# The recurrence over chunks is moved from beside attention to beside the input projections

## The chip, the cores and the metric

The kernel runs on one core of a Trainium2 chip. The metric is the device time of one execution in microseconds (us). The core has five engines that take their own instruction queues in order: TensorE (PE, its weight loads are shown as PEld), VectorE (DVE), ScalarE (ACT), GpSimd (POOL) and SyncE (SP), which here only issues DMAs. Matrix products land in PSUM, eight banks, and ScalarE or VectorE must take them out of there.

## The reference

One layer on 2048 tokens of width 1024. A normalised input goes through one combined projection; half of the columns feed eight heads of softmax attention with a forget bias, the other half eight heads of a recurrence (RWKV-7). Both results side by side go through an output projection, and a gated feed-forward layer follows.

```python
u = rmsnorm(h, attn_norm_pre)
proj = u @ w_in
o_fox = forgetting_attention(fq, fk, fv, ff, fox_forget_bias)
# recurrence, S is 64x64 per head, one step per token:
S = S * w_t + (S a_t) b_t^T + v_t k_t^T
y_t = S r_t
# its norm per head and its gate
o_rwkv = (norm(y) * ln_w + ln_b + bonus) * g
h = h + rmsnorm(concat(o_fox, o_rwkv) @ w_out, attn_norm_post)
h = h + rmsnorm((silu(z @ w_gate) * (z @ w_up)) @ w_down, ffn_norm_post)
```

## The kernel before

**Stages.** The 2048 tokens are four blocks of 512. `phase_a` makes the input projections of a block in turn, 27 products of 128 columns each: three small latent ones (`stage_l`), twelve for the recurrence (`stage_pre`, four pairs of heads with three each) and twelve for attention (`stage_fox`). A product (`proj`) is 24 matmuls of 512 columns: operands are split into a high and a low part, and three products of parts are added (`mm3`). The weights come new for every product and block: a load of 512 KB (`wraw`, L187), a cast on ScalarE (`wh`, L217), a subtraction on GpSimd (`wl`, L218), each with three buffers. The normalised and transposed input of a block (`uh`, `ul`) has two buffers, one for each of two blocks in turn. `stage_pre` leaves five operands of the recurrence for each chunk of 64 tokens in memory (`A5`, stored as `scr["a5"]`), and `stage_solve` inverts the chunks' triangular matrices on VectorE and leaves them in `scr["td"]`.

`phase_b` runs three lanes side by side: the recurrence (`rwkv`), attention (`attention`), and the output projection of the blocks that are done (`Mix.block`, with `Mix.norm` behind it). The feed-forward part (`Ffn`) comes last; the output projection of the fourth block runs beside its first loads.

**The recurrence.** It works in groups of two chunks and four heads; four groups are a half block (four of the eight heads), two half blocks a block, 32 groups in all. A group has ten steps: `tt` twice (transposes, L669, L670), `gram` twice (G, L681, masked by VectorE at L684), `x` (X, L692), `u` (U, L700), `c` twice (C, L708) and `y` twice (Y, L725), where VectorE multiplies the state (`SI`, L726) and ScalarE copies the result into `yg` (L728). Each step ends with copies out of PSUM by ScalarE or VectorE. Steps of two neighbouring groups are interleaved by the list `ORDER`; a dash marks a step of the group before. Every group loads its operands (`A`, L636, `PL`, L637) and its inverses (`TD`, L647) through SP's queue. After four groups `post_norm` gives norm and gate of two pairs of heads in three steps each, called "tail" in `ORDER`.

**Attention.** A unit is one head and 256 queries (J counts them, 0 to 7; two units of a head for each block of 512), 64 units in all, 16 in a block. `scores` makes S (L886, L887), adds the bias while taking the maximum on VectorE (L894) and the exponential on ScalarE (L900). `values` transposes the result (L929), splits it (L935, L937) and multiplies by V into O (L947). VectorE adds O's two halves into `ot` (L953), which has one buffer; GpSimd scales it and stores it (L954, L955). The scores of a unit run beside the values of the one before.

**What sets the order.** `weave` takes generators and steps through them in proportion to the length given with each one (a third number scales it); what comes first in the program has the higher priority. The framework then plans the order on each engine, and inserts the waits. `behind` gives the output projection a much lower priority. A block's output projection starts when the recurrence has finished the block (`rdone`) and attention has begun the next one (`adone`).

Of the kernel before, what the change touches and what calls it, by code (L numbers as in the profile page):

```python
# [10 lines left out]
F32 = mybir.dt.float32  # L11
# [4 lines left out]
ALU = mybir.AluOpType  # L16
# [20 lines left out]
ORDER = ("t0", "-c0", "tail", "t1", "-c1", "tail", "g0", "-y0", "g1", "load", "-y1", "x", "tail", "u", "tail")  # L37
# [117 lines left out]
def phase_a(k, tc, ins, scr):  # L155
# [5 lines left out]
    with ExitStack() as ctx:  # L161
# [17 lines left out]
        spare = p1.tile([128, 2, D], F32, tag="A5", name="spare", bufs=2)  # L179
# [14 lines left out]
        fetched = [fetch(L0 + 128, 128), fetch(L0 + 256, 72), fetch(L0, 128)]  # L194
# [17 lines left out]
        def weights(c0, n):  # L212
            raw = fetched.pop(0) if fetched else fetch(c0, n)
# [32 lines left out]
        def start_block(b, blk):  # L246
            blk.b, blk.t = b, slice(b * BT, (b + 1) * BT)
            blk.uh = pu[b % 2].tile([128, NJ, BT], F32R, tag="uh", name="uh")
            blk.ul = pu[b % 2].tile([128, NJ, BT], F32R, tag="ul", name="ul")

        def flip(blk, tt, xt):
            for jj in range(2):
# [4 lines left out]
                cols = slice(tt * 128, (tt + 1) * 128)  # L257
                oh = blk.uh[:, jj * 4:jj * 4 + 4, cols]
# [3 lines left out]
        def first_u(blk):  # L262

            start_block(0, blk)
            for i, xt in enumerate(first_x):
# [12 lines left out]
        def stage_u(b, blk):  # L278
            start_block(b, blk)
            prev = None  # L280
# [68 lines left out]
        def stage_pre(blk, p, nd, pl):  # L349
# [5 lines left out]
            A5 = p1.tile([128, NCB, 5, CL], F32, tag="A5", name="A5", bufs=2)  # L355
# [154 lines left out]
        def stage_fox(blk, i):  # L510
# [3 lines left out]
            oh = p2.tile([128, BT], F32R, tag="fo", name="oh", bufs=3)  # L514
            ol = p2.tile([128, BT], F32R, tag="fo", name="ol", bufs=3)
# [11 lines left out]
            else:  # L527
                vt = p2.tile([128, BT], F32, tag="fo", name="vt", bufs=3)
# [4 lines left out]
                vs = p2.tile([128, 4, 2, 2, HD], F32R, tag="vs", name="vs")  # L533
# [21 lines left out]
        weave((stage_l(blk), 3))  # L555
# [12 lines left out]
        weave((solve, NSOLVE), (fox, 6))  # L568


def rwkv(k, tc, ctx, ins, scr):

    nc = tc.nc
    pa = ctx.enter_context(tc.tile_pool(name="r_a", bufs=2))
    cp = ctx.enter_context(tc.tile_pool(name="r_const", bufs=1))
    p2 = ctx.enter_context(tc.tile_pool(name="r2", bufs=2))
    ps_rw = ctx.enter_context(tc.tile_pool(name="r_rw", bufs=2, space=PSUM))

    pg = ctx.enter_context(tc.tile_pool(name="r_g", bufs=1, side="right"))
    g1 = pa.tile([128, HW], F32, tag="bv0", name="g1", bufs=1)  # L580
    nc.scalar.dma_start(out=g1, in_=ins["rwkv_g_up"][0][0:128, :])
    g2 = pa.tile([128, HW], F32, tag="bv1", name="g2", bufs=1)
# [1046 lines left out]
```

## Time and profile before

| | us |
|---|---|
| median of 3 runs | 3539.27 (3529.62 to 3541.76) |
| the profiled execution | 3532.8 |
| its span | 3531.0 |
| TensorE busy | 3107.4 (88%) |
| VectorE busy | 2424.2 (69%) |
| ScalarE busy | 1542.2 (44%) |
| GpSimd busy | 1511.0 (43%) |
| mean granted TensorE clock | 0.922 |

The granted clock is the share of TensorE's full rate that it was given; in the records it has two levels, 1 (2.4 GHz) and one half (1.2 GHz), and a mean between them says how much of a stretch was at which. Matmuls are pipelined, so that the length of one record is longer than the distance to the next. Busy shares over the whole span mix the stages, which have different limits; a stage has to be read in its own window.

### The profile page before, as it was taken

To read this page: it belongs to the slowest core of one execution; us is meant where nothing else is said; L and a number is where in the kernel's file an instruction comes from. 1 tells how busy PE (TensorE), PEld (TensorE's weight loads), DVE (VectorE), ACT (ScalarE), POOL (GpSimd) and SP (SyncE) were. 2 spreads that over 40 slices of the span, in tenths; PEclk is the share of its full clock that TensorE was granted. 3 is DMA by queue.
4 is the path that set the end of the run, shared out by engine and by line. 5 is a ranking of instruction groups with operands and counts; after the bars stand their busy time and mean duration, and the time that the engine had idled before them with its cause. 6 is when DMAs were issued, how large, how long until landed. Compare 5 with 4: busy or idle time off the path is not lost. (4 is left out here: it accounts for less than half of the span.)

```text
span 3531.0 us, 48961 instructions
## 1 busy us (share of the span) xinstructions
PE 3107.4 (88%) x16657; PEld 2566.7 (73%) x16657; DVE 2424.2 (69%) x5285; ACT 1542.2 (44%) x2966; POOL 1511.0 (43%) x1203
## 2 busy tenths in 40 slices
PE   7999999994678889898888779999999999997895
PEld 5777777773567778687777657888878888775674
DVE  6877666664245666657666557687685556999898
ACT  5444444332445555555655343333333333543432
POOL 3343444442322232223223245343453334887776
PEclk9999999997688989898998789999999999998898
DMA  4766566577546666656664563243232222322321
GB/s 127 189 169 174 152 168 174 158 174 172 106 108 131 159 147 158 133 157 178 169 172 117 154 212 117 101 150 114 84 119 84 84 78 107 144 98 93 143 96 72
DMA packets 509198, 480.31 MB, mean 136 GB/s; under 512 B 143780, under 2 KB 410070, under 8 KB 506902
## 3 DMA queue, kind: packets, MB, share of 16 engines
q1 hardware_dynamic: 473734, 432.47, 43.0%
q0 software_dynamic: 11008, 24.20, 2.7%
q10 hardware_dynamic: 24208, 20.52, 1.9%
q8 instruction: 133, 2.18, 0.3%
q14 instruction: 115, 0.94, 0.1%
HBM read 350.25 MB, written 126.81 MB: 135 GB/s over the span
## 5 line engine op out<-in xcount | busy, mean ns | idle before, releaser
L1196 POOL TENSOR_TENSOR wl<-fraw,wh 128x512 fp32r<-128x512 f32 x132 | 186.5, 1414 | 474.5 <-ACT wh L1192 458.1
L218 POOL TENSOR_TENSOR wl<-wraw,wh 128x1024 fp32r<-128x1024 f32 (+1 forms) x108 | 262.2, 2430 | 297.3 <-ACT wh L217 292.8
L1440 POOL TENSOR_TENSOR dop<-draw,dop 128x512 fp32r<-128x512 f32 x210 | 330.3, 1602 | 92.8 <-ACT dop L1438 53.8
L1192 ACT CAST wh<-fraw 128x512 fp32r<-128x512 f32 x308 | 187.4, 618 | 387.7 <-PE gp L77 198.3
L76 PE MATMUL mm<-uh,wh 128*128 128x512 f32 (+1 forms) x864 | 348.7, 404 | 1.4 <-DVE ol L522 1.4
L78 PE MATMUL mm<-uh,wl 128*128 128x512 f32 (+1 forms) x864 | 346.8, 401 | 0.0
L77 PE MATMUL mm<-ul,wh 128*128 128x512 f32 (+1 forms) x864 | 346.1, 401 | 0.0
L76 PE MATMUL dps<-dop 128*128 128x512 f32 x624 | 251.6, 408 | 57.8 <-ACT acc L1535 27.8
L1438 ACT CAST dop<-draw 128x512 fp32r<-128x512 f32 x280 | 155.7, 622 | 234.5 <-DVE draw L1446 152.7
L77 PE MATMUL dps<-dop 128*128 128x512 f32 x624 | 248.1, 398 | 1.2 <-POOL dop L1440 1.2
L78 PE MATMUL dps<-dop 128*128 128x512 f32 x624 | 246.7, 397 | 0.0
L947 PE MATMUL O<-th,Vs 128*128 128x256 f32 (+1 forms) x672 | 202.1, 355 | 39.4 <-DVE ot L953 19.7
L76 PE MATMUL gp<-za,wh 128*128 128x512 f32 x528 | 210.1, 398 | 15.8 <-ACT za L1192 9.9
L929 PE MATMUL pt<-ident,P 128*128 128x128 f32 x1088 | 191.5, 300 | 31.4 <-DVE tl L937 22.4
L1196 DVE TENSOR_TENSOR wl<-fraw,wh 128x512 fp32r<-128x512 f32 x176 | 157.5, 895 | 85.9 <-ACT wh L1192 82.0
L937 DVE TENSOR_TENSOR tl<-pt,th 128x512 fp32r<-128x512 f32 (+2 forms) x280 | 163.1, 590 | 72.6 <-ACT th L935 68.8
L77 PE MATMUL gp<-za,wh 128*128 128x512 f32 x528 | 208.1, 394 | 2.8 <-DVE za L1196 2.8
L78 PE MATMUL gp<-za,wl 128*128 128x512 f32 x528 | 208.7, 395 | 0.0
L894 DVE CUSTOM_DVE_ANT_0 P<-S,ng 128x512 f32<-128x512 f32 (+3 forms) x288 | 169.4, 596 | 52.5 <-PE S L887 27.7
L1446 DVE TENSOR_TENSOR draw<-draw 128x512 f32<-128x512 f32 x160 | 194.5, 1232 | 5.3 <-POOL dop L1440 4.7
L76 PEld LDWEIGHTS mm<-uh,wh 128*128 128x128 f32 (+1 forms) x864 | 165.8, 192 | 43.4 <-issue 3.8
L900 ACT ACTIVATE P<-P,nmx 128x128 f32<-128x128 f32 (+15 forms) x128 | 154.1, 1205 | 96.7 <-DVE nmx L899 75.7
(362 smaller groups left out, 8568.9 us busy)
## 6 DMA issues: line engine op xcount, KB each, us to landing
wraw<-in_w_in SPq DMA_DIRECT2D x104, 512.0 KB
fraw<-in_ffn_w_gate SPq DMA_DIRECT2D x22, 1024.0 KB
fraw<-in_ffn_w_up SPq DMA_DIRECT2D x22, 1024.0 KB
scr_hid<-s SPq DMA_DIRECT2D x22, 1024.0 KB
draw<-scr_hid SPq DMA_DIRECT2D x22, 1024.0 KB
draw<-in_ffn_w_down SPq DMA_DIRECT2D x22, 1024.0 KB
scr_a<-A SPq DMA_DIRECT2D x16, 1280.0 KB
A<-scr_a SPq DMA_DIRECT2D x64, 320.0 KB
```

Of the source, the lines that this page charges most:

```text
L76: nc.tensor.matmul(out, lhsT=wh, rhs=xh, start=first, stop=False)
L77: nc.tensor.matmul(out, lhsT=wh, rhs=xl, start=False, stop=False)
L78: nc.tensor.matmul(out, lhsT=wl, rhs=xh, start=False, stop=last)
L218: nc.gpsimd.tensor_tensor(wl[:, :, 0:m], raw[:, :, 0:m], wh[:, :, 0:m], op=ALU.subtract)
L894: nc.vector.tensor_tensor_reduce(out=P[:, c0 + a:c0 + e], in0=S[:, a:e], in1=bias, op0=ALU.add, op1=ALU.max, scale=1.0, scalar=-3.0e38, ac ...
L929: nc.tensor.transpose(pt[:, e, qi, :], Ps[qi][:, kb * 128:(kb + 1) * 128], k.ident)
L937: nc.vector.tensor_tensor(tl[:, w[0], w[1]], pt[:, w[0], w[1]], th[:, w[0], w[1]], op=ALU.subtract)
L947: nc.tensor.matmul(O[:, q0 * 128:QB], lhsT=vv, rhs=p[:, e, q0:NQ, :], start=kb == 0 and i == 0, stop=kb == nkb - 1 and i == len(parts) - 1)
L1192: f.nc.scalar.copy(h, x)
L1196: e.tensor_tensor(l[:, c], x[:, c], h[:, c], op=ALU.subtract)
L1440: e.tensor_tensor(r[1][p][i], x, r[0][p][i], op=ALU.subtract)
L1446: V.tensor_tensor(o[p], x[p], y[p], op=op)
```

## The change

The recurrence becomes a class with a generator for each half block, and `phase_a` steps through half block n - 2 while it projects half block n. Half block 6 runs beside the last products of attention's operands, half block 7 in `phase_b`. Norm and gate become a class of their own, `Gates`, which stays in `phase_b` and runs block by block as a lane of its own; between the two, the recurrence's result `yg` goes through memory (`scr["ry"]`). `phase_a` has fewer buffers, in SBUF and PSUM: weights from three to two, the product's PSUM banks and those of the elementwise steps from three to two each, `A5` from two to one, and `uh`, `ul` from two to one: the next block's input is kept unsplit (`us`) and split at the border (`split`). Attention's projections (`stage_foxes`) run in the same half block and no more one half block later, except in the last block, and the latent ones (`stage_l`) at a block's start instead of at the end of the block before. Attention's tiles move to the other side of SBUF.

```diff
-ORDER = ("t0", "-c0", "tail", "t1", "-c1", "tail", "g0", "-y0", "g1", "load", "-y1", "x", "tail", "u", "tail")
+ORDER = ("t0", "-c0", "t1", "-c1", "g0", "-y0", "g1", "load", "-y1", "x", "u")
+ORDER0 = ("load0", "-c0", "-c1", "-y0", "t0", "-y1", "t1", "g0", "g1", "load", "x", "u")
...
-        pu = [ctx.enter_context(tc.tile_pool(name=f"a_u{i}", bufs=1)) for i in range(2)]
-        pw = ctx.enter_context(tc.tile_pool(name="a_w", bufs=3))
+        pu = ctx.enter_context(tc.tile_pool(name="a_u", bufs=1))
+        pw = ctx.enter_context(tc.tile_pool(name="a_w", bufs=2))
...
-        ps_el = ctx.enter_context(tc.tile_pool(name="a_el", bufs=3, space=PSUM))
-        ps_mm = ctx.enter_context(tc.tile_pool(name="a_mm", bufs=3, space=PSUM))
+        ps_el = ctx.enter_context(tc.tile_pool(name="a_el", bufs=2, space=PSUM))
+        ps_mm = ctx.enter_context(tc.tile_pool(name="a_mm", bufs=2, space=PSUM))
...
+        def split(blk):
+
+            operands(blk)
+            for j in range(NJ):
+                nc.scalar.copy(blk.uh[:, j], blk.us[:, j])
+                (nc.vector if j % 2 == 0 else nc.gpsimd).tensor_tensor(blk.ul[:, j], blk.us[:, j], blk.uh[:, j], op=ALU.subtract)
...
-            A5 = p1.tile([128, NCB, 5, CL], F32, tag="A5", name="A5", bufs=2)
+            A5 = p1.tile([128, NCB, 5, CL], F32, tag="A5", name="A5")
...
             for half in range(2):
+                n = b * 2 + half
                 nd = dr.tile([32, CL, CL], F32, tag="nd", name="nd")
-                lanes = [(chain(*(stage_pre(blk, half * 2 + pl, nd, pl) for pl in range(2))), 14), (solve, NSOLVE), (fox, 6)]
+                pre = [stage_pre(blk, half * 2 + pl, nd, pl) for pl in range(2)]
+                if half == 0:
+                    if b > 0:
+                        split(blk)
+                    pre = [stage_l(blk)] + pre
+                if b + 1 < NB:
+                    fox = stage_foxes(blk, half * 6)
+                lanes = [(chain(*pre), 17 if half == 0 else 14), (solve, NSOLVE), (fox, 6)]
                 if half == 1 and b + 1 < NB:
-                    lanes.append((chain(stage_u(b + 1, nxt), stage_l(nxt)), 8))
+                    lanes.append((stage_u(b + 1, nxt), 5))
+                if n >= 2:
+                    lanes.append((rec.half(n - 2), 40))
                 weave(*lanes)
-                solve = stage_solve(nd, scr["td"][b * 2 + half])
-                fox = stage_foxes(blk, half * 6)
+                solve = stage_solve(nd, scr["td"][n])
+                fox = stage_foxes(blk, half * 6) if b + 1 == NB else iter(())
             blk = nxt
-        weave((solve, NSOLVE), (fox, 6))
+        weave((solve, NSOLVE), (fox, 6), (rec.half(NB * 2 - 2), 40))
...
+            if g == NG - 1 and q == 1:
+                for e in range(2):
+                    nc.gpsimd.dma_start(out=o.scr["ry"][i // (2 * NG), half * 2 + e], in_=o.yg[e].rearrange("p g h d -> p (g h d)"))
...
+    def half(o, n):
+
+        NG = o.NG
+        for i in range(n * NG, (n + 1) * NG):
+            for step in ORDER0 if i % NG == 0 else ORDER:
+                lag = step[0] == "-"
+                if step == "load0":
+                    o.load(i)
+                    o.groups.append(o.group(i))
+                elif step == "load":
+                    if i % NG < NG - 1:
+                        o.load(i + 1)
+                        o.groups.append(o.group(i + 1))
+                elif i >= lag:
+                    o.groups[i - lag][step[lag:]]()
+                    yield
...
+    def block(o, b, done):
...
+        for p in range(4):
+            yg = p2.tile([128, NCB // 2, 2, HD], F32, tag="yg", name="yg")
+            nc.sync.dma_start(out=yg.rearrange("p g h d -> p (g h d)"), in_=scr["ry"][b, p])
...
-        weave((recurrence(rdone), NB * (8 * 10 + 13), 0.92), (after(), 560 * T // 2048), (run(adone), n_at))
+        first = chain(*(gates.block(b, rdone) for b in range(NB - 1)))
+        last = chain(rec.half(NB * 2 - 1), rec.flush(), gates.block(NB - 1, rdone))
+        weave((last, 44 + 16, 0.6), (first, 16 * (NB - 1), 0.25), (after(), 560 * T // 2048), (run(adone), n_at))
```

## Rows read from the trace of the kernel before

**Rows 1.** Windows by stage: window, length, busy us of PE, PEld, DVE, ACT, POOL; clock, DMA

```profile
100.00:800.00 700.00, 662.14 (x4085) 531.06 (x4084) 488.52 (x1186) 302.04 (x492) 316.48 (x223) 0.96 0.65 168
837.00:1034.00 197.00, 128.89 (x797) 110.43 (x797) 65.57 (x299) 80.51 (x233) 53.93 (x75) 0.71 0.54 105
1034.00:1212.00 178.00, 147.52 (x985) 131.38 (x985) 106.18 (x392) 95.34 (x230) 48.30 (x71) 0.90 0.61 133
1212.00:1524.00 312.00, 273.64 (x1787) 239.83 (x1788) 199.51 (x640) 174.30 (x370) 87.62 (x106) 0.89 0.62 153
1524.00:1944.00 420.00, 371.69 (x2467) 329.08 (x2468) 272.04 (x858) 236.59 (x485) 122.21 (x134) 0.91 0.56 156
1944.00:2030.00 86.00, 63.56 (x329) 52.30 (x328) 50.14 (x168) 33.31 (x72) 23.35 (x24) 0.74 0.52 154
2030.00:3531.00 1501.00, 1369.68 (x5801) 1102.27 (x5800) 1161.55 (x1531) 562.93 (x987) 815.99 (x533) 0.96 0.32 111
```

**Rows 2.** Timeline, end of attention, recurrence; first feed-forward weight: start, length, what

```profile
1942.82 0.22 PE L947 MATMUL O<-th,Vs 128*128 128x128 f32 x1
...
2004.81 1.97 PE L725 MATMUL Y<-SI,CS 128*128 128x64 f32 x8 [0.74 <-DVE SI L726]
...
2027.66 0.38 SPq L1186 DMA_DIRECT2D fraw<-in_ffn_w_gate  x1
```

**Rows 3.** Waits between 795 and 900 us: who, for whom, total us, times, longest

```profile
PE S L886 <- DMA Q<-scr_qS: 22.0, 2, 20.3
```

**Rows 4.** Timeline of TensorE, one group of the recurrence among other work

```profile
1660.94 0.27 PE L669 MATMUL tt<-ident,A 128*128 128x128 f32 x1
...
1661.38 1.06 PE L708 MATMUL C<-R,UV 128*128 128x128 f32 x8
...
1672.41 1.16 PE L681 MATMUL G<-A 64*128 64x128 f32 x8
...
1677.18 1.00 PE L725 MATMUL Y<-SI,CS 128*128 128x64 f32 x8
...
1683.12 0.73 PE L692 MATMUL X<-UV,R 64*64 64x64 f32 x16
...
1689.19 1.06 PE L700 MATMUL U<-Z,TD 128*128 128x128 f32 x8
```

**Rows 5.** Groups by line, 837 to 2030: count, busy us, mean ns, idle before

```profile
L728 ACT COPY yg<-Y 64x128 f32<-64x128 f32 x128 | 26.7, 257 | 66.7 <-DVE SI L726 66.1
...
L684 DVE TENSOR_TENSOR R<-G,gmask 128x256 f32<-128x256 f32 x128 | 48.1, 417 | 13.6 <-PE G L681 12.2 <-issue 0.6
...
L953 DVE TENSOR_TENSOR ot<-O,ol 64x256 f32<-64x256 f32 x64 | 26.5, 414 | 109.9 <-DMA scr_mixT<-ot 77.0 <-ACT ol L952 18.0 <-issue 7.8
```

**Rows 6.** Weights in the projections: groups by line; waits of SP's queue

```profile
L217 ACT CAST wh<-wraw 128x1024 fp32r<-128x1024 f32 (+1 forms) x108 | 111.4, 1032 | 139.6 <-PE mm L77 72.5 <-issue 31.0 <-POOL Tt L461 15.6
...
SPq L187 <- POOL wl L218: 73.4, 30, 4.4
```

**Rows 7.** Timeline of SP's queue: loads of TD for one group

```profile
960.08 2.75 SPq L647 DMA_DIRECT2D TD<-scr_td  x4
```

**Rows 8.** Windows as in 1; then groups by line: 1367 to 1447, 1447 to 1524

```profile
1367.00:1447.00 80.00, 75.21 (x530) 65.67 (x528) 56.06 (x176) 48.05 (x104) 21.78 (x26) 0.98 0.68 158
1447.00:1524.00 77.00, 58.30 (x347) 51.51 (x348) 47.18 (x167) 37.63 (x76) 14.83 (x21) 0.76 0.55 142
1637.00:1738.00 101.00, 98.71 (x710) 87.48 (x709) 66.99 (x209) 62.18 (x130) 24.32 (x29) 1.00 0.65 179
1738.00:1838.00 100.00, 81.66 (x526) 71.90 (x525) 69.52 (x240) 55.28 (x111) 25.61 (x31) 0.86 0.61 167
...
L725 PE MATMUL Y<-SI,CS 128*128 128x64 f32 x48 | 6.1, 270 | 0.6 <-ACT yg L728 0.6
...
L725 PE MATMUL Y<-SI,CS 128*128 128x64 f32 x24 | 4.7, 365 | 0.0
...
L953 DVE TENSOR_TENSOR ot<-O,ol 64x256 f32<-64x256 f32 x4 | 1.6, 411 | 0.0
```

More of the change, by code (lines that the diff above doesn't have):

```diff
@@ L192, in fetch @@
             return raw
-        fetched = [fetch(L0 + 128, 128), fetch(L0 + 256, 72), fetch(L0, 128)]
+        fetched = {c0: fetch(c0, n) for c0, n in ((L0 + 128, 128), (L0 + 256, 72))}
         wa_h = [cp.tile([128, HW], F32R, name=f"wa_h{i}") for i in range(2)]
@@ new lines, in phase_a, with __init__, bank, load @@
+        weave((solve, NSOLVE), (fox, 6), (rec.half(NB * 2 - 2), 40))
+class Recurrence:
+    def __init__(o, k, tc, ctx, scr):
+        nc = tc.nc
+        o.k, o.nc, o.scr = k, nc, scr
+        o.pa = ctx.enter_context(tc.tile_pool(name="r_a", bufs=2))
+        cp = ctx.enter_context(tc.tile_pool(name="r_const", bufs=1))
+        o.p2 = ctx.enter_context(tc.tile_pool(name="r2", bufs=2))
+        o.ps = ctx.enter_context(tc.tile_pool(name="r_rw", bufs=2, space=PSUM))
+        o.gmask = cp.tile([128, 2, CL], F32, name="gmask")
+        nc.gpsimd.memset(o.gmask, 1.0)
+        for h in range(2):
+            for q in range(2):
+                ap = o.gmask[h * 64:(h + 1) * 64, q, :]
+                nc.gpsimd.affine_select(out=ap, in_=ap, pattern=[[1, CL]], compare_op=ALU.is_gt if q == 0 else ALU.is_ge,
+                                        fill=0.0, base=0, channel_multiplier=-1)
+        o.SI, o.TD, o.UV = [], [], []
+        for half in range(2):
+            t = cp.tile([128, 2, 2, HD], F32, name=f"SI{half}")
+            nc.gpsimd.memset(t[64:128], 0.0)
+            for u in range(4):
+                nc.gpsimd.tensor_copy(t[0:64, u // 2, u % 2, :], k.ident[0:64, 0:64])
+            o.SI.append(t)
+        for i in range(2):
+            t = cp.tile([128, 2, 2, 128], F32, name=f"TD{i}")
+            nc.gpsimd.memset(t, 0.0)
+            o.TD.append(t)
+        for i in range(2):
+            t = cp.tile([128, 2, 2, 2, 128], F32, name=f"UV{i}")
+            nc.gpsimd.memset(t[64:128], 0.0)
+            o.UV.append(t)
+        o.NG = NCB // 2
+        o.groups = []
+    def bank(o, n):
+        return o.ps.tile([128, 4, 128], F32, tag="rw", name=n)
+    def load(o, i):
+        nc, scr, NG = o.nc, o.scr, o.NG
@@ L719, in y @@
             if g == 0 and q == 0:
-                for pr in prs:
-                    pr.yg = p2.tile([128, NG, 2, HD], F32, tag="yg", name="yg")
+                o.yg = [p2.tile([128, NG, 2, HD], F32, tag="yg", name="yg") for e in range(2)]
             Y = bank("Y")[:, 0:2, :].rearrange("p e (h d) -> p e h d", h=2)
@@ L814, in run @@
+            nc.sync.dma_start(out=scr["mixT"][HW + p * 128:HW + (p + 1) * 128, t], in_=om)
             yield
-    return run
+        done[0] = b
 def attention(k, tc, ctx, scr):
@@ L1102, in behind, with phase_b @@
         yield
-def phase_b(k, tc, ins, scr, mix):
+def phase_b(k, tc, ins, scr, mix, rec):
     T = k.T
@@ L1110, in phase_b @@
     with ExitStack() as ctx:
-        recurrence = rwkv(k, tc, ctx, ins, scr)
+        gates = Gates(k, tc, ctx, ins, scr, rec.ps)
         ps_e = ctx.enter_context(tc.tile_pool(name="e_p", bufs=1, space=PSUM))
         run = attention(k, tc, ctx, scr)
-        rdone, adone = [0], [0]
+        rdone, adone = [-1], [0]
         def after():
@@ L1579, in fox_rwkv7_block @@
     constants(k, tc, ctx, ins)
-    phase_a(k, tc, ins, scr)
     NB = T // BT
     with ExitStack() as c2, ExitStack() as ce:
-        mix = Mix(k, tc, ce, ins, scr)
-        phase_b(k, tc, ins, scr, mix)
+        with ExitStack() as cr:
+            rec = Recurrence(k, tc, cr, scr)
+            phase_a(k, tc, ins, scr, rec)
+            mix = Mix(k, tc, ce, ins, scr)
+            phase_b(k, tc, ins, scr, mix, rec)
         ffn = Ffn(k, tc, c2, ins, scr, out[0])
```

207 lines of the change are left out of this document (69 added, 138 removed).

## The prediction

> **What bounds the kernel now.** I read the stretches of the span first, because the shares on the page mix four different stages. [rows 1] has one window for each: the input projections (100 to 800 us), attention over its four blocks of 512 queries (837 to 1034, 1034 to 1212, 1212 to 1524, 1524 to 1944), what is left of the recurrence when attention has ended (1944 to 2030), and the feed-forward part (2030 to 3531). The reader is to look at PE busy and at the granted clock together. I call PE busy times granted clock the *work*, in microseconds at full speed, and work divided by the window's length the *density*. The projections have 662.1 x 0.96 = 636 us of work in 700, a density of 0.91: TensorE bounds them, and no other engine is over 70% (VectorE, 488.5). The five windows from 837 to 2030 have 91.5 + 132.8 + 243.5 + 338.2 + 47.1 = 853 us of work in 1193, a density of 0.715. The worst are the first block (0.46) and the end (0.55); blocks 2 and 3 stand at 0.78 and 0.81. So a microsecond of TensorE work is cheaper to place beside the projections than beside attention, and that is the whole question of this change: TensorE's work is not made less, it is moved to a stage with another density.
>
> Second, the end. The last matmul of attention starts at 1942.82, the last one of the recurrence at 2004.81, and the first load of a feed-forward weight, which needs what attention, recurrence and gate hold, goes out at 2027.66 [rows 2]. These 85 us exist because the recurrence with its gate is the longer of two lanes. Third, the start: TensorE stands still for 20.3 us before attention's first scores, until Q has landed [rows 3].
>
> **What moves, and its work.** The recurrence has 32 groups (8 half blocks of 4). The 28 of half blocks 0 to 6 go beside the projections; the last four, all norms and all gates stay. [rows 4] shows each step's burst at full clock: tt (records 0.11 us apart, eight of them in a group: 0.88), C 1.06 twice, G 1.16 twice, Y 1.00 twice, X 0.73, U 1.06, together 9.1 us. A record lasts 0.27 and the next starts 0.11 after it, so each of the eight other bursts ends some 0.16 after the next could begin: 7.8 us at least. 28 groups are 218 to 255 us; I take 8.6 a group, 240.
>
> **Cost in the projections.** At their own density of 0.91 the 240 us take 240 / 0.91 = 264. Less is possible, if the steps fall into TensorE's idle 38 us of the 700 (bound: 218 less 8 of these 38, 210). The other engines have room: the recurrence's costliest VectorE group is 48.1 us for all 32 groups [rows 5] and it has four such groups, so under 4 x 48.1 x 7/8 = 168 come to the 488.5, and the stretch grows by more. ScalarE is at 43%.
>
> The same edit takes buffers away, since the recurrence's tiles now live through this stage. Raw and split weights go from three buffers to two. Today the weight cast, 1.03 us each, waits 72.5 us in all for TensorE to free a buffer, and the fetch on SP's queue waits 73.4 us in 30 waits for the subtraction that frees its own [rows 6]: the fetch is limited by buffers and not by bandwidth, and one less takes one projection's lead away. I price that at nothing to 0.8 us (most of a cast) for each of the 81 projections of blocks 1 to 3, 0 to 65, and take none, because the cast is short and the moved steps lengthen the time between projections that hides it. The normalised input is now held once: at three block borders ScalarE and VectorE must split the first slice while TensorE waits, a cast of half the weight cast's size, so some 0.52, and a subtraction that takes longer: I allow 3 us each, 9 in all. The 24 casts, some 13 us, lie on a ScalarE with room. Moved past SP's queue are the loads: four of TD take 2.75 us of issue [rows 7], so 28 x 2.75 = 77 and about as much for A and PL; behind them stand weight fetches, and a load that waits for its buffer holds the fetch behind it; this risk is in the 65. The state's output goes out and comes back through memory, 16 tiles of 256 KB; the gate runs a block behind, which hides it. Sum: 264 + 9 = +273, bounds +210 and +338.
>
> **Gain in attention.** 853 - 240 = 613 us of work stay. At the old density of 0.715 they take 857, at 0.70 876. What the density will be no row shows directly, so I look at both sides. For a better one: the two worst windows shrink. The end goes, since four groups and one block's gate are done well before attention ends. Recurrence steps also block the in-order queues of other engines: ScalarE's copy of Y has 66.1 us of waiting for the state's update in front of it [rows 5]. For a worse one: the first block is not short of engines, its VectorE waits 77.0 us over the whole of attention for the store of the unit before, through the one *ot* buffer [rows 5], so there the recurrence was free filling. And the filling of blocks 2 and 3 goes too: [rows 8] has two pairs of neighbouring stretches of four attention units each. With 48 records of Y (three groups) the density is 75.2 x 0.98 / 80 = 0.92; with 24 it is 58.3 x 0.76 / 77 = 0.58, and four units take 77 us instead of 80. In block 3 it is 0.98 against 81.7 x 0.86 / 100 = 0.70, again in the same time. I take 0.70: between the average and the sparse stretches, nearer to the average because the end and the blocked queues are gone. 876 us, a gain of 317, with bounds 0.78 (786, gain 407) and 0.56 (1095, gain 98; worked out below).
>
> **Sum.** 3531 + 273 - 317 = 3487 us of span. The profiled run took 3532.8, 1.8 more than its span, and the median of the runs is 0.18% above it: 3489 x 1.0018 = 3495.
>
> **Rivals,** as spans; a median is 8 us more. *Attention keeps its pace* (slower). Place: attention's blocks 1 to 3, 910 us. Mechanism: with less on TensorE its clock falls, matmuls take twice as long, and four units take what they took. For it: in both sparse stretches of [rows 8] the clock is lower (0.76 and 0.86 against 0.98 and 1.00), and the time the same. Against it: these stretches still carry recurrence steps, norms and gates in the queues of the other engines. Price: first block 175 (the start a little shorter), blocks 1 to 3 still 910, end 10: 1095, gain 98, 3531 + 273 - 98 = 3706. It decides from the point where the gain falls below 273: blocks 1 to 3 over 735, that is four units of block 2 over 63 us. Half-way (0.9 of today's pace) gives 3615.
>
> The Trainium skill, page "TensorE: Matmul & The Clock Gate", section "Why this matters for your kernels", speaks for this rival: it asks to avoid idle gaps between bursts of matmuls, since the array then goes back to half its rate. The clock of 0.76 in the sparser stretch agrees. By that rule alone, with the clock of that stretch and 0.80 busy, 613 us take 613 / 0.61 = 1005, and the change costs 85.
>
> *Both stages do better.* The moved steps fill the projections' idle time (+210) and attention, with the other queues freed, reaches 0.78, block 2's own density today: gain 407. 3531 + 210 - 407 = 3334. For it speak the waits in [rows 5]; against it that the sparse stretches show no faster unit.
>
> *The projections starve.* Two weight buffers don't cover the fetch, and TensorE, the bound there, waits 0.8 us a projection: +338, gain 317 as forecast, 3552. For it: the 73.4 us in [rows 6]; against it: the cast waits for TensorE and not TensorE for the cast.
>
> **How the numbers follow.** Forecast 0.48, own range 3420 to 3550; attention keeps pace or nearly 0.24 (3560 to 3715); both better 0.18 (3340 to 3420); starving 0.10 (3540 to 3590); all as medians. A measurement of this kernel tells about 0.3% from no change, 3529 to 3550 here. Faster: 0.39 of the forecast's, 0.18 and 0.01: 0.58. Same: 0.05 of the forecast's, 0.03 of the third and 0.02 of the first rival: 0.10. Slower: 0.32. For eight in ten the range goes from 3385, a good half of the better case, to 3630, half of the slower one.
>
> **What would show it.** In the profile after, the projections should end near 1110 instead of 837, with a density of about 0.91 from 100 us on; if the stretch is longer and TensorE's idle time there is ended by the weight cast or subtraction, the two buffers are to blame. Attention's last matmul to the first feed-forward weight load should be under 20 us instead of 85. Four units of block 2 should take under 63 us, four of block 3 under 85; if they take 77 and 100 with a clock of 0.8 or less, the slower rival holds. The feed-forward part should be 1501 us as before. The forecast is wrong if the density of either stage moves by over 0.05 from 0.91 and 0.70.

## The result and the profile after

The change makes the kernel slower: a median of 3634.9 us (3619.3 to 3637.9) against 3540.5 for the kernel before, a ratio of 1.0256 with a 95% interval of 1.0211 to 1.0302. The forecast was 3495, within 3385 to 3630. The profiled execution after has a span of 3635.3 us, 104 more than before.

The windows of the kernel after, as in [rows 1]: projections, the step to attention, attention's four blocks of 512 queries, and the feed-forward part (us, TensorE, its weight loads, VectorE, ScalarE, GpSimd busy and records, granted clock, DMA share, GB/s).

```profile
100.00:1022.00 922.00, 875.44 (x5851) 717.51 (x5850) 618.27 (x1500) 442.29 (x885) 336.65 (x237) 0.95 0.57 151
1022.00:1047.00 25.00, 20.36 (x239) 17.74 (x238) 5.34 (x14) 12.39 (x33) 4.14 (x6) 0.76 0.64 162
1047.00:1269.00 222.00, 147.40 (x787) 126.32 (x785) 88.66 (x380) 86.58 (x247) 65.52 (x89) 0.73 0.68 130
1269.00:1514.00 245.00, 189.12 (x1063) 161.54 (x1063) 155.40 (x503) 107.54 (x241) 98.85 (x120) 0.87 0.72 156
1514.00:1819.00 305.00, 220.21 (x1159) 180.24 (x1160) 168.54 (x599) 137.35 (x245) 92.77 (x109) 0.86 0.61 160
1819.00:2133.00 314.00, 245.11 (x1380) 204.47 (x1380) 181.91 (x563) 155.18 (x258) 80.17 (x96) 0.88 0.54 139
2133.00:3635.00 1502.00, 1372.00 (x5825) 1104.75 (x5824) 1176.57 (x1573) 565.36 (x993) 817.49 (x536) 0.96 0.33 113
```

Attention's first scores come at 1047 instead of 837: +210. From there to the feed-forward part it takes 1086 instead of 1193: only 107 come back, of which the end's 85 are the larger part. Its four blocks take 222, 245, 305 and 314 us; before they took 197, 178, 312 and 420 [rows 1]. So the first two became slower and only the last one got much faster. The feed-forward part is as it was.

How many groups of the recurrence run where is read from the matmuls of its last step (Y, 16 records a group), the same windows with that line alone (TensorE, weight loads, clock, DMA share, GB/s), after:

```profile
0.00:1022.00 1022.00, 45.59 (x336) 44.79 (x336) 0.96 0.57 152
1022.00:1047.00 25.00, 3.07 (x16) 2.75 (x16) 0.76 0.64 162
1047.00:1269.00 222.00, 16.03 (x96) 15.90 (x96) 0.73 0.68 130
1269.00:1514.00 245.00, 9.28 (x64) 9.61 (x64) 0.87 0.72 156
1514.00:1819.00 305.00, 0.00 (x0) 0.00 (x0) 0.86 0.61 160
```

and before:

```profile
837.00:1034.00 197.00, 11.73 (x64) 11.22 (x64) 0.71 0.54 105
1034.00:1212.00 178.00, 12.09 (x80) 11.62 (x80) 0.90 0.61 133
```

336 + 16 records are 22 groups ahead of attention, not 28. The other ten, 96 + 64 records, run beside blocks 0 and 1, where before there were nine (64 + 80). These two blocks lost nothing. They gained the gates: the norm's first reduction with its scaling (`mn`, two VectorE records for each of 16 pairs of heads) falls wholly into them (VectorE, GpSimd, clock, DMA share, GB/s; after):

```profile
1047.00:1269.00 222.00, 5.49 (x10) 5.20 (x5) 0.73 0.68 130
1269.00:1514.00 245.00, 13.98 (x22) 11.75 (x11) 0.87 0.72 156
```

Before, two pairs lay in each of these blocks. The new waits there are those of the gates' transfers (waits of the kernel after, 1047 to 1514: who, for whom, total us, times, longest):

```profile
DVE mn L797 <- DMA yg<-scr_ry: 62.3, 13, 9.2
DVE ot L958 <- DMA scr_mixT<-ot: 45.2, 14, 6.5
...
POOL bv L792 <- DMA scr_mixT<-bv: 41.8, 9, 12.1
```

The end went as planned: attention's last matmul starts at 2132.6 at the latest, the first load of a feed-forward weight at 2138.2 (one tile's records: shortest, median, longest ns, first and last start):

```profile
L952 PE MATMUL O<-tl,Vs x14: 278/326/475, 2120.3 to 2132.6; 128*128 128x256 f32 x13, 128*128 128x128 f32 x1
...
L1193 SPq DMA_DIRECT2D fraw<-in_ffn_w_gate x1: 378/378/378, 2138.2 to 2138.2; - x1
```

### The profile page after: what moved, and what is told of

It reads as the page before. It is cut to its first block, busy times and chain, and to the rows that moved or that the text cites. A ratio compares the mean times of both kernels' runs of the same rounds, so it can differ in the third digit from the quotient of the medians.

```text
span 3635.3 us, 49041 instructions
## 1 busy us (share of the span) xinstructions
PE 3148.3 (87%) x16657; PEld 2574.7 (71%) x16657; DVE 2450.7 (67%) x5263; ACT 1559.1 (43%) x2990; POOL 1540.0 (42%) x1241
## 5 line engine op out<-in xcount | busy, mean ns | idle before, releaser
L952 PEld LDWEIGHTS O<-th,Vs 128*128 128x128 f32 x672 | 147.2, 222 | 106.1 <-ACT th L940 52.0
L940 ACT CAST th<-pt 128x512 fp32r<-128x512 f32 (+2 forms) x280 | 137.8, 509 | 173.8 <-PE pt L934 109.6
L891 PE MATMUL S<-Ks,Q 128*128 128x512 f32 (+2 forms) x320 | 146.3, 460 | 73.2 <-DVE mx L899 44.0
L77 PEld LDWEIGHTS mm<-uh,wh 128*128 128x128 f32 (+1 forms) x864 | 167.5, 194 | 57.6 <-issue 11.3
```

What stands on the lines that cost most here:

```text
L77: nc.tensor.matmul(out, lhsT=wh, rhs=xh, start=first, stop=False)
L891: nc.tensor.matmul(S[:, 0:n], lhsT=Q1[:, qs], rhs=hd.Ks[c0 // 512][:, 0:n], start=True, stop=False)
L952: nc.tensor.matmul(O[:, q0 * 128:QB], lhsT=vv, rhs=p[:, e, q0:NQ, :], start=kb == 0 and i == 0, stop=kb == nkb - 1 and i == len(parts) - 1)
```

## The experiments

Each run is told by its stages: attention's first scores, then the length of its four blocks, each up to VectorE's last `ot`. The theories are named by letters where an expectation first states them; the first three are that the lanes that stayed hold attention up (Q), that attention keeps its own pace whatever lies beside it (P, the rival of the prediction without its cause), and that the clock sets it (C). Two cautions. The time varies from run to run and from chip to chip: 20 executions of the kernel before on one chip lay between 3558 and 3598, and its medians on the chips used between 3540 and 3579. Most of this is attention's length, since the first scores (832 to 837 in three versions of the kernel before) and the feed-forward part (1489 to 1510 from its first weight load to the end, in all runs) hardly move. So single profiles whose stages differ by less than some 40 us are taken as equal; h3, h4, h6 and h8 ran on a chip on which the kernel before took 3554, most others on chips on which it took 3579. And "alone" still has five groups of the recurrence (four in h4) beside block 0, those of half blocks 5 and 6 that had not ended. The end is the time from attention's last `ot` to the first load of a feed-forward weight; where the table has none, it is under 6 us.

| run | first scores | blocks 0 to 3 | sum | groups beside | ratio to before (95%) |
|---|---|---|---|---|---|
| before | 837 | 197, 178, 312, 420 | 1107 + end 83 | 32, 3 of them in the end | 1 |
| after | 1047 | 223, 245, 305, 314 | 1087 | 10 | 1.0256 (1.0211 to 1.0302) |
| a1_attention_alone | 1119 | 203, 175, 216, 261 | 855 | 5 | |
| a2_attention_mix | 1063 | 207, 205, 295, 308 | 1016 | 5 | |
| a5_no_mix | 1098 | 241, 214, 249, 259 | 962 | 10 | |
| a3_spread | 1043 | 221, 247, 310, 320 | 1099 | 10 | 1.0186 (1.0152 to 1.0220) |
| b1_after_two_ot | 1044 | 174, 222, 373, 355 | 1123 | 10 | 1.0225 (1.0201 to 1.0250) |
| b2_alone_two_ot | 1121 | 173, 181, 219, 269 | 843 | 5 | |
| b3_alone_fill | 1127 | 208, 195, 242, 280 | 925 | 5 | |
| b4_before_two_ot | 832 | 163, 207, 347, 447 | 1163 + end 120 | 32, 4 of them in the end | 1.0126 (1.0086 to 1.0165) |
| c0_none_moved | 910 | 210, 219, 319, 425 | 1173 | 27 | 1.0032 (1.0009 to 1.0054) |
| c2_two_moved | 957 | 229, 231, 346, 344 | 1151 | 23.5 | 1.0091 (1.0052 to 1.0131) |
| f1_mix_matmuls | 1120 | 203, 200, 240, 260 | 902 | 5 | |
| d1_before_08 | 833 | 218, 183, 340, 423 | 1164 + end 84 | 32, 3 of them in the end | 1.0005 (0.9981 to 1.0028) |
| h3_fill_copies | 1116 | 206, 177, 240, 283 | 907 | 5 | |
| h4_copies | 1145 | 177, 178, 222, 258 | 835 | 4 | |
| h6_alone_two_o | 1115 | 169, 179, 210, 262 | 821 | 5 | |
| h8_alone_loads_once | 1118 | 190, 157, 171, 205 | 722 | 5 | |
| i2_alone_loads | 1121 | 211, 163, 249, 253 | 876 | 5 | |
| i5_alone_steps | 1117 | 214, 197, 251, 296 | 958 | 5 + 27 | |

The late first scores of the runs that leave work out are the copies that put other data in its place, not the lanes: there the first product of the projections already starts late, at 34 to 81 us instead of 26.

**What stands beside attention.** Lanes left out, or the gates spread:

```diff
-        weave((last, 44 + 16, 0.6), (first, 16 * (NB - 1), 0.25), (after(), 560 * T // 2048), (run(adone), n_at))
+        weave((run(adone), n_at))                                        # a1
+        weave((after(), 560 * T // 2048), (run(adone), n_at))            # a2
+        weave((last, 60, 0.6), (first, 48, 0.25), (run(adone), n_at))    # a5
+        weave((last, 44, 0.4), (first, 16 * NB, 0.9), (after(), 560 * T // 2048), (run(adone), n_at))  # a3, first: 4 blocks
```

> The changed kernel with nothing beside attention: the last half block of the recurrence, all norms and gates and the output projection of blocks 0 to 2 are left out (other data stand in their place in memory). Theory Q (the lanes that stayed hold attention up, in the in-order queues): attention runs all through at the pace of its fastest stretches after the change, some 54 us for four units in block 2 and 50 to 58 in block 3, so about 150 + 150 + 216 + 220 = 740 us instead of 1086, span about 3290. Theory P (attention keeps its pace because its own chain of waits sets it, whatever lies beside it): about 1000 to 1090, span 3550 to 3635. Theory C (the clock: with less beside it TensorE falls to half rate and attention gets slower still): over 1090, with a granted clock under 0.75.

> The changed kernel with attention and the output projection of blocks 0 to 2 alone: the last half block of the recurrence and all norms and gates are left out. Theory Q, if gates and the last half block are to blame: blocks 0 and 1 run at 150 each, and the projection's 768 matmuls (about 130 us of TensorE time at full clock) fill gaps in blocks 1 to 3: 740 to 850 us, span 3290 to 3400. Theory Q, if the output projection is to blame: blocks 2 and 3 stay at 305 and 314, some 920, span 3470. Theory P: 1000 to 1090.

> The changed kernel with attention, the last half block of the recurrence and all norms and gates, without the output projection of blocks 0 to 2. Theory Q, if the gates and the half block are to blame: blocks 0 and 1 stay near 222 and 245, blocks 2 and 3 go to 216 and 220, sum about 900, span 3450. If the output projection is to blame: blocks 0 and 1 fall by little and blocks 2 and 3 as far. Theory P: 1000 to 1090 in all four blocks as after the change.

> The changed kernel with the gates spread over attention: one lane for the gates of all four blocks at 0.9 of attention's length instead of three blocks' gates in its first quarter, and the last half block of the recurrence over the first 0.4. Nothing is left out. Theory Q: blocks 0 and 1 lose VectorE's 62 us of waits for yg out of memory and GpSimd's 42 us of waits for the gate's own store, and take 175 to 190 each instead of 222 and 245; blocks 2 and 3 take some of it back. Time 3540 to 3590, against 3635. Theory P: no change, 3620 to 3650.

Attention alone takes 855 us, between theories Q and P. Theory C falls: it asked for over 1090 with less beside attention, and attention became shorter, at a clock of 0.69 to 0.89. The output projection adds 161, half block 7 with the gates 107: together 268, against 232 between a1 and the changed kernel (244 to a3, on the chip of a1), so the prices nearly add up, and neither lane is hidden. Spreading the gates changes no block beyond the noise (by its ratio a3 may be up to 1% better than the changed kernel, the intervals hardly overlap), so their crowding in the first two is not what costs; they cost about the same elsewhere. The floor is what matters: a1's windows (columns as in the first block above) show attention alone at a density, work to length, of 0.56 (128.2 x 0.69 + 111.5 x 0.81 + 150.7 x 0.84 + 197.7 x 0.89 = 481 in 855).

```profile
1118.00:1322.00 204.00, 128.23 (x672) 109.29 (x671) 62.48 (x296) 78.10 (x228) 54.43 (x76) 0.69 0.59 111
1322.00:1497.00 175.00, 111.50 (x564) 91.68 (x562) 73.78 (x292) 68.44 (x148) 39.60 (x62) 0.81 0.47 106
1497.00:1713.00 216.00, 150.66 (x884) 124.46 (x885) 126.22 (x423) 99.73 (x183) 41.28 (x64) 0.84 0.53 113
1713.00:1974.00 261.00, 197.68 (x1158) 162.15 (x1157) 157.93 (x484) 128.48 (x212) 40.80 (x63) 0.89 0.47 106
```

**Buffers of ot, and TensorE's own time.** Two buffers for `ot` and `rb`; 280 steps of transposes of a constant:

```diff
-        u.rb = p1.tile([64, QB], F32, tag="rb", name="rb")
+        u.rb = p1.tile([64, QB], F32, tag="rb", name="rb", bufs=2)
-        ot = p1.tile([64, QB], F32, tag="ot", name="ot")
+        ot = p1.tile([64, QB], F32, tag="ot", name="ot", bufs=2)
...
+                t = rec.bank("dm")
+                for q in range(8):
+                    nc.tensor.transpose(t[:, q % 4, :], k.ident, k.ident)
```

> The changed kernel with two buffers instead of one for attention's result ot and for the reciprocal rb that scales it (room comes from the norm's squares, which go to PSUM). Theory R (the chain of ot sets a unit's pace: VectorE's add waits until the unit before has been scaled and stored, 11 to 13 us a unit in blocks 0 and 1 of the run with attention alone, and TensorE's O waits for that add): blocks 0 and 1 fall from 222 and 245 to about 190 each, blocks 2 and 3 by 10 to 20 each, time 3520 to 3570 against 3635. If the chain is only one of several limits of the same length: no more than 20 us, 3610 to 3640.

> The run with attention alone (855 us from its first scores to its last result: 203, 175, 216, 261) with two buffers for ot and rb. Last half block, norms, gates and output projection of blocks 0 to 2 are left out as there. Theory R: blocks 0 and 1 fall to 100 to 140 each, blocks 2 and 3 to 190 and 240, sum under 720. If attention alone is bound by its scores' chain (Q load, maximum, exponential, transposes) or by the clock: over 820.

> The run with attention alone (855 us) and beside it 280 steps of eight transposes of a constant into PSUM, about 8 x 0.11 + 0.16 = 1.0 us of TensorE time a step at full clock, 280 us in all, as much as the moved recurrence steps, with no other engine and no DMA in them. What attention's lanes compute is left out as there. Theory P (TensorE's time beside attention is free, since the pace is set by waits): 855 to 900, with a granted clock over 0.90. Theory W (work adds up whatever the waits): 1050 to 1135. Half-way, 900 to 1050, would say how much of a step finds a gap.

> The kernel before with two buffers for ot and rb, room made in the same way. Theory R: its block 0 (197 us, 77 us of VectorE waits for the store of ot over all of attention) falls to about 150, the others by little since the recurrence fills their waits; the end of the stage is set by the recurrence, which runs at its own weight of 0.92: 3500 to 3540 on a chip where before is 3540. If the other lanes set the pace: same within 0.3%.

Theory R falls: the buffers shorten block 0 by 30 to 49 us, and that is not kept. Alone the sum is the same (843). In the changed kernel blocks 2 and 3 take 68 and 40 us more, and nothing is gained that can be measured. The kernel before loses 1.3%: its four blocks together take as long as d1's (1163 and 1164; d1, below, is timed equal to the kernel before), and its end is 120 us instead of 84.

The constant steps cost attention 70 us. Their windows:

```profile
1127.00:1335.00 208.00, 135.48 (x782) 118.86 (x779) 61.11 (x287) 76.89 (x225) 53.81 (x75) 0.72 0.62 107
1335.00:1530.00 195.00, 171.08 (x1259) 159.54 (x1260) 71.14 (x284) 68.01 (x142) 40.40 (x63) 0.93 0.49 89
1530.00:1772.00 242.00, 228.51 (x1819) 214.71 (x1818) 134.09 (x441) 106.29 (x188) 41.20 (x64) 0.99 0.44 106
1772.00:2052.00 280.00, 234.95 (x1653) 208.56 (x1651) 161.66 (x483) 127.70 (x210) 40.73 (x63) 0.94 0.40 100
```

That is 704 us of work against 481: 223 us more TensorE work in 70 us more time, 0.3 for one. Block 2 has a granted clock of 0.99 instead of 0.84, yet takes 242 us instead of 216. This alone does not part the clock from the waits, since TensorE is busy for 228.5 of these 242 us, the constant steps included; h8 below does.

**How many groups are moved.** The changed kernel with the recurrence beside the projections up to half block K only, the rest and the gates as one lane of 0.92; and the kernel before with a shorter lane:

```diff
-                if n >= 2:
+                if 2 <= n < K + 2:
...
+        weave((lane(), 40 * (2 * NB - K) + 4 + 16 * NB, 0.92), (after(), 560 * T // 2048), (run(adone), n_at))
...
-        weave((recurrence(rdone), NB * (8 * 10 + 13), 0.92), (after(), 560 * T // 2048), (run(adone), n_at))
+        weave((recurrence(rdone), NB * (8 * 10 + 13), 0.8), (after(), 560 * T // 2048), (run(adone), n_at))
```

> The changed kernel with all its restructuring (the class, gates as a lane of their own with the recurrence's result through memory, the fewer buffers, the split borders), but with all eight half blocks of the recurrence beside attention and none beside the projections. Nothing is left out. It parts the price of the fewer buffers from that of the moved steps. Theory P: the projections end where they did before, 837 plus 9 for three borders plus little for two weight buffers: first scores at 840 to 860, so that the other 190 to 200 of the +210 belong to the moved steps; beside attention the same 28 groups cost only 70 to 110 more than the 1087 of the changed kernel, some 1160 to 1200; time within 1% of the kernel before. If the buffers are what costs: first scores at 880 to 950. Theory W (work adds up in attention as it does in the projections): attention 1290 and more, time 3630 and up.

> The changed kernel with only half blocks 0 and 1 beside the projections and six beside attention; nothing is left out. Theory P with the steps at 7.5 us a group in the projections and 2.5 to 4 us beside attention: 60 us more for the projections, 20 to 32 less for attention, 30 to 40 slower than with none moved, unless the recurrence's lane ends first and its end (86 us before) goes: then 20 to 50 faster than with none moved.

> The kernel before with the recurrence's lane weighted 0.80 and not 0.92 of attention's length, so that it should end earlier. If the 86 us between attention's last result and the recurrence's end are a lane that was planned too late, and filling is nearly free: attention ends 10 to 30 later, the end falls to under 30, time 3490 to 3530 on a chip where before is 3540 (0.3 to 1.4% faster). If the recurrence is limited by its own chain or the planner's order: same within 0.3%.

In c0 the planner of the order itself took five groups ahead into the projections, so it is a point at 5 groups moved, c2 one at 8.5, the changed kernel one at 22 (c0: Y alone in its windows):

```profile
0.00:870.00 870.00, 9.29 (x64) 9.46 (x64) 0.96 0.60 159
870.00:909.00 39.00, 2.18 (x16) 1.94 (x16) 0.69 0.75 216
909.00:2083.00 1174.00, 63.15 (x432) 61.16 (x432) 0.87 0.66 147
```

c0's first scores thus miss the 840 to 860 of its expectation, in part by these five groups. From c0 to after, the first scores come 138 us later for 17 groups: 8.1 us a group (the way by c2 splits unevenly: 47 for 3.5, then 91 for 13.5). The projections' last product starts at 870 in c0 and at 1022 after, which would be 8.9 a group. At 8.1, c0's +72 are 41 for its five groups and 32 for the rest; that is an estimate, and the rest is more than the fewer buffers and the split borders: the last 128 matmuls of the inverses (`xp`, `yp`) run behind the first scores in the kernel before (at 862 to 864 the last ones) and ahead of them here. Attention gives back 86 for the 17, 5.1 a group. By the timed ratios, each taken on one chip with the kernel before, c0 and after differ by 2.2%, 80 us, so attention gave back 138 - 80 = 58, or 3.4 a group; by their medians, from two chips, they differ by 43, which leaves 95, or 5.6 a group. The time rises with every group moved: 1.0032, 1.0091, 1.0256 (the last from another chip). And the end is gone in c0 too (4 us), with 27 groups still beside attention. Weighting the lane of the kernel before at 0.80 changes nothing (d1): timed they are equal, so the 57 us by which attention is longer in d1's profile are a difference between chips and runs and not the weight's, and the end did not shrink.

**Where a lane's price lies.** The output projection's matmuls alone (f1); copies with the constant steps (h3) and without (h4); the groups' loads alone (i2) and their steps without loads (i5):

```diff
+                if b == 3:                       # f1: only here load, copy out, store
...
+                nc.scalar.copy(fa, t)            # h3: behind the eight transposes
+                nc.vector.tensor_tensor(fd, t[:, 0:2], fd, op=ALU.mult)
...
+                    rec.load(i)                  # i2: 28 times
...
+            rec.load = lambda i: None            # i5: then half blocks 0 to 6 once more
```

> Attention with the matmuls of the output projection of blocks 0 to 2 alone: its operands are loaded and split once, and its loads, its later weights, its copies out of PSUM, its stores and its norm are left out, and so are the last half block, norms and gates. With attention alone the stage took 855 us, with the whole output projection 1016. If TensorE's time is what the output projection costs there: 980 to 1020. If its transfers and its work on the other engines' queues cost it, and its 130 us of matmuls find gaps as the constant transposes did (70 us for some 250): 870 to 910.

> The run with attention alone (855 us; beside it still the last five groups of half block 6) and 280 steps like those of b3_alone_fill, each now with the two copies that a recurrence step makes: ScalarE copies the bank out of PSUM (128 x 512) and VectorE multiplies half of it. Theory Q (a step's price beside attention lies in the in-order queues of ScalarE and VectorE): 855 + 28 x 5.9 = 1020, that is 990 to 1050, against 925 with TensorE's part alone. If the copies cost nothing: 920 to 945.

> The same 280 steps without TensorE: two ScalarE copies (128 x 256) and one VectorE multiply (128 x 256) a step between constant tiles in SBUF, that wait for no other engine. If the engines' time costs by itself: 920 to 1000. If only a copy that waits in the queue for its matmul holds others up: 855 to 890.

> Attention alone (855 us) and beside it the loads of 28 groups of the recurrence (A, PL and TD, some 0.9 MB a group) with no step that uses them. Theory D (transfers set the pace beside attention: those of K, V, bias and Q and those of the other lanes stand in one queue): 855 + 80 to 140, that is 935 to 995. If only a load that waits for its buffer holds the queue, and not the transfer itself: 855 to 890.

> Attention alone and beside it all steps of 28 groups of the recurrence without their loads (operands of one group in place, so the values are not those of the reference). Theory D: 855 + 40 to 90, as the constant steps with copies (907): 895 to 945. If the chain of a step over TensorE, ScalarE and VectorE is what costs attention: 855 + 120 to 165, 975 to 1020.

The output projection's matmuls cost 47 us of its 161; the other 114 are its loads, casts, copies, stores and norms together, which were not parted further. For the recurrence it is the other way: its loads cost 21, which is no difference, the copies none that can be told from the chips' difference (907 against 925, 835 against 855), its whole steps 103 for 27 groups. 103 + 21 are 4.6 us a group, within the 3.4 to 5.6 from above. Theories Q and D both fall for the recurrence: a group has no dear part beside attention; the largest of what was tried is TensorE's time (the 70 us of the constant steps), and that is cheap too.

**What paces attention alone.** Two PSUM banks for O with the two buffers (h6); K, V and bias loaded for one head in eight (h8):

```diff
-    ps_o = ctx.enter_context(tc.tile_pool(name="b_o", bufs=1, space=PSUM))
+    ps_o = ctx.enter_context(tc.tile_pool(name="b_o", bufs=2, space=PSUM))
...
-                hd = load_head(h, b)
+                hd = load_head(h, b if h == 0 else -1)
+                if h == 0:
+                    held = hd
+                hd.Ks, hd.Vs, hd.ng = held.Ks, held.Vs, held.ng
```

> Attention alone with two buffers for ot and rb (843 us) and two PSUM banks for O as well, so that the next unit's O can start before the one before has been taken out. If the chain behind O sets attention's pace: under 780. If the scores' chain does, or the order on the engines: 825 to 860.

> Attention alone, with K, V and bias loaded for the first head of each block only and used by all eight (seven of eight loads of them left out; the Q loads stay). If these loads set attention's pace: under 780, most of it in blocks 2 and 3, where a head needs three and four pieces of each and there are five buffers. If not: 835 to 860.

The chain behind O is worth 34 us, in block 0, which is within the noise. The loads are worth 133, of which 101 in blocks 2 and 3, whose windows then read:

```profile
1465.00:1636.00 171.00, 144.74 (x886) 116.97 (x887) 126.47 (x425) 99.38 (x183) 41.79 (x65) 0.95 0.26 46
1636.00:1840.00 204.00, 179.70 (x1152) 147.31 (x1151) 157.02 (x480) 126.07 (x211) 40.77 (x63) 0.97 0.15 31
```

These two windows also answer for the clock. It rose, from 0.84 and 0.89 to 0.95 and 0.97. But of the 102 us that they are shorter than a1's, 78 are time in which TensorE had stood idle (65 to 26 and 63 to 24), and only 24 are a shorter busy time (151 to 145, 198 to 180). So with attention alone the low clock is mostly a sign of its waits and not what sets its pace.

The waits say the same. With attention alone (1497 to 1974):

```profile
DVE ngm L881 <- DMA ng<-scr_nc: 69.0, 14, 9.9
PE S L896 <- DMA Ks<-scr_kS: 26.5, 8, 6.3
```

and with the loads once (1465 to 1840):

```profile
DVE ngm L881 <- DMA ng<-scr_nc: 5.6, 1, 5.6
```

The loads seem to be late because they wait for buffers. The queue that issues them in order stands for the matmuls that still read V (L865) and for the scores that still read the Q of an earlier unit (L877; SP's queue, a1, 1497 to 1974):

```profile
SPq L865 <- PE O L957: 84.4, 38, 14.1
SPq L877 <- PE S L897: 65.7, 7, 11.0
```

That transfers by themselves are cheap here, i2 shows (21 us for 28 groups' loads); a run with more buffers was not made, so the cause stays argued. The Trainium skill, page "Perfetto Trace Analysis", section "Optimization Strategy", says that the same gap coming again and again, on an engine that should be saturated, can mean too little room for the next tile; the 38 waits of the first row agree, for tiles of V, though they are the issuing queue's. What paces blocks 0 and 1 (157 and 190 us even then) stays open.

## Why the prediction was wrong

**The bound.** Right for the projections: after, they have 875.4 x 0.95 / 922 = 0.90 of work to length, and a group of 8.6 us of work cost 8.1 to 8.9 (forecast 264 / 28 = 9.4). The stage bound by TensorE sells its time at nearly full price.

**28 groups.** Wrong: 22 went. The prediction counted the steps from the program's order and did not ask whether the last half blocks, which depend on the newest operands and are woven into the last products, would end in time (that this is why they were left behind is read from the program and was not tried). With 22 groups its own terms give 22 x 9.4 + 9 = 216 for the projections; measured are +210, which are 22 x 8.1 = 178 and 32. So the +210, which was the lower bound, came from the smaller number. That it came out at the bound is luck. For the fewer buffers and the borders it had 9, with 65 more as a bound; the estimate of 32 is inside. *The projections starve* is not seen: TensorE's idle time is 46.6 of 922 us, 5%, where it was 37.9 of 700.

**The end.** Right in size: 85 us became 6, and the feed-forward part stayed (1502, forecast 1501). But it did not need the move: c0, where 27 groups stay beside attention and the gates are a lane of their own, has an end of 4 us, and four blocks of 1173 us in all.

**The density of what stays.** This is the step that failed. The prediction took 613 us of work at 0.70, between the stage's average and its sparse stretches, 876 us and a gain of 317; measured are 1086 us and a gain of 107. The windows after have 677 us of work (147.4 x 0.73 + 189.1 x 0.87 + 220.2 x 0.86 + 245.1 x 0.88; six groups more than forecast are 52 of the 64), at a density of 0.62. The first error is small: 677 at 0.70 would be 967, not 1086. The second is of kind: density was treated as a property of the stage that work carries away when it leaves. But 855 of the 1087 us are left with nothing but five groups beside attention (a1), and a group that leaves takes only its marginal price with it: 107 / 22 = 4.9 us by the two profiles, 3.4 to 5.6 by c0, 4.6 by i2 and i5, where the prediction had 317 / 28 = 11.3. The warning stood in [rows 8]: with half the Y matmuls, four units took as long. The prediction quoted these pairs and then chose 0.70 against them.

As a sum: 22 x (8.1 - 4.9) + 32 = 102, measured 104, of which 1 is the feed-forward part. It closes because its terms come from the same two profiles; the prices from c0, i2 and i5 are what supports it.

A term put at nothing was the recurrence's result on its way through memory, which the gates' running a block behind was to hide: VectorE waits 62.3 us for it in blocks 0 and 1. What that costs is open, since spreading the gates changed no block.

**The rival** *Attention keeps its pace* had the right price (gain 98, measured 107) by the wrong road. It put the pace into blocks 1 to 3 and the cause into the clock. In fact the groups left the late blocks: block 3 fell by 106 and the first two rose by 25 and 67. Four units of block 2 took 97, 83, 54 and 71 us, of block 3 96, 90, 71 and 58, where the forecast needed under 63 and 85. And the clock is at most a small part of the cause: attention alone became shorter at about the same clock or a lower one, and where blocks 2 and 3 got shorter in h8, three quarters were TensorE's idle time. Its total, 3706, missed because it kept 28 groups' cost in the projections. *Both stages better* failed with attention's density.

Of the rule on idle gaps that the prediction weighed, the half on the clock held: filling raised it from 0.84 to 0.99 in block 2. What the higher clock bought there can't be told from what the filling took. The cost of 85 that the prediction worked out by it came near the measured 104 by luck: it had 28 groups at 273, and attention at a clock of 0.76 with TensorE busy 0.80; measured are 22 groups at 210, and clocks of 0.73 to 0.88 with TensorE busy 0.74 (801.8 of 1086). A rule that would have spoken against the change stands in the Trainium skill, page "Perfetto Trace Analysis", section "Optimization Strategy": stages with different limits may gain from being interleaved. The kernel before had just that, steps that need TensorE beside a stage that waits for its loads, and the prices of 8.1 beside the projections and 4.9 beside attention agree.

**Open.** Why the first two blocks became slower by as much as they did: the prices of the gates add up there, and `mn` and `bv` wait 62 and 42 us for transfers, but spreading the gates did not help. What part of the output projection's 114 us lies in which of its operations was not tried. Whether more buffers for attention's loads would shorten it was not tried. No run that computes everything was faster than the kernel before.

## What to carry to other kernels

Before moving work between two stages, price it at the margin in both: leave it out of the one (or double it there) and read that stage's length, not its busy share. In a stage that TensorE bounds, moved work costs its full time; in a stage paced by loads and chains of waits, taking it away gives back a part only, here some 40 to 70%, and its low clock and low density then belong to what stays. And read from the trace how many of the moved steps really run in the new place, since a planned order may leave the last ones behind.

## What was not expected of the hardware

A higher granted clock and a shorter stage are two things. With the constant steps beside it block 2 had a clock of 0.99 and took 242 us, at 0.84 216. With K, V and bias loaded once it had 0.95 and took 171, and 39 of these 45 us were TensorE's idle time.

Copies from memory to memory delayed the whole kernel from its very start. The program has them at the second block of the projections, but in the planned order GpSimd issues them at 7 to 11 us. TensorE's first product then starts at 33.6 us with 4 MB (a2), at 66.5 with 15 MB (a5) and at 80.1 with 19 MB (a1), instead of 26.4, and attention's first scores come 15, 50 and 71 us later. 7, 40 and 54 us of that are there at the first product. The stretch from 25 to 50 us, after and in a1 (columns as in the first block above), and in a1 the issue of the first copy and the first product:

```profile
25.00:50.00 25.00, 25.00 (x107) 19.00 (x106) 6.00 (x15) 10.12 (x15) 10.55 (x7) 1.00 0.44 113
...
25.00:50.00 25.00, 0.00 (x0) 0.00 (x0) 0.00 (x0) 0.00 (x0) 0.00 (x0) 1.00 1.03 337
...
L573 POOL DMA_DIRECT2D scr_mixT<-in_x x1: 689/689/689, 7.0 to 7.0; - x1
...
L77 PE MATMUL mm<-uh,wh x864: 387/389/793, 80.1 to 1092.2; 128*128 128x512 f32 x168, 128*72 128x512 f32 x5
```
